# Mixer products halved panel by panel with more of them ahead of two waits, and seven squares in each down-projection sweep

## The chip, the cores and the metric

The kernel runs on one core of a Trainium2 chip. That core has five engines that each run their own list of instructions: TensorE (PE in the profile; PEld is its loading of the stationary operand), VectorE (DVE), ScalarE (ACT), GpSimd (POOL) and SyncE (SP), which here only issues DMAs. They wait for each other through semaphores. PE reads SBUF and writes PSUM, which has eight banks of 512 floats in each of 128 partitions; ACT and DVE read PSUM and write SBUF.

The metric is the time of one execution in microseconds, the median over several runs. One per cent of the time before is 12.1 us.

## The reference

One layer of a decoder trunk on 256 tokens of width 2048. A mixer with two kinds of heads, a squared-ReLU MLP of width 8192, and a gated embedding:

```python
h = rms_norm(x, attn_norm)
z = h @ w_in                         # 4096 + 288 columns
zs = token_shift(z[pool part left out], mu_shift)
pool_out = (windowed means of z_pool, minus z_pool) @ pool_w * pool_scale
rwkv_out = rwkv7_time_mix(r, k, v, w, a, g from zs)
x = x + concat(pool_out, rwkv_out) @ w_out
h2 = rms_norm(x, mlp_norm)
x = x + square(relu(h2 @ w_ffn_up)) @ w_ffn_down
gate = sigmoid(rms_norm(x, ple_norm) @ w_ple_gate)
x = x + gate * (p @ w_ple_proj)
return rms_norm(x, final_norm)
```

The time mixing has a recurrence over tokens, S = S diag(w) + (S a) b^T + v k^T, y = S r, for 16 heads of 64. All is float32.

## The kernel before

**Products in parts.** A float32 product is made of three matmuls on rounded parts. A weight panel of 128 x 1024 (two k-tiles of 512 columns) is loaded as `raw`, ACT writes its rounded high part `wh` (two operations of 512 columns) and DVE the rest, `wl = raw - wh` (one operation of 1024 columns); this is `split_w`, L160 to 167. With activations split the same way, a product is high x high, high x low and low x high. Panels live in rings of three buffers in the mixer, and of four from the MLP on (`ring`, L147). A panel is loaded again into a buffer when the last reader of the old one is done.

**The mixer, from 26 us of the profile on.** The order of PE's instructions is the written order here (`manual_schedule` for PE); ACT's and DVE's order is a planner's, which simulates the program and picks by priority. Eight products with `w_in` (zk0, zr0, zk1, zr1, zv0, zv1, zp0, zp1) are generators in one queue. Each step of a generator emits one small product and tells a nominal time: 0.36 us in `gemm_cols` (three matmuls of 256 columns, L177 to 180; 64 steps) and 0.68 in `gemm_toks` (three of 512, L187 to 189; 32 steps). `fill(us)` takes steps from the queue until so much nominal time is emitted, and `finish(gen)` until a generator is through. Between the fills stands the recurrence in chunks of 64 tokens, for two groups of eight heads: `rwkv_lora` and `rwkv_k` (keys, their norms with `rnq` and `rnb`, and the operand AR, L588 to 594), the scores (`sc`, L623, and for group 1 L652, in halves of two parts), `inverse` (31 steps of two DVE operations that invert 32 x 32 triangles), `rwkv_merge` (joins the 32-blocks to 64, `gm` L740 and `qm` L749, out of T1G), `rwkv_values`, and `rwkv_core`, four chunks each of which needs the one before (`us` L842, its copies UV L849 on ACT and L850 on DVE, the state L857, the outputs `dy` L870). `inverse` is itself a generator: `pace` emits one of its 38 pieces for every 1.0 us of queue time, and `while beside: fill(1.0)` runs it to its end ahead of the merge.

The panels of a queued product go one after the other, except at the ends: `apart` merges the first two panels and the last two (L191), and within a merged group all steps of output half 0 come before those of half 1. In between, each k-tile goes through half 0 and half 1 in turn. When half 0 of the last group is complete, `consume` reads its PSUM bank out (`shift_evac`: ACT L332, DVE L333, for four pieces). Products share three PSUM banks, so the next product's half 1 takes the bank of this one's half 0.

Behind the core: `pool_chunk`, the first token half's group_out, `fill(4.0)`, the second one's (`yt` L902), the gates of each group with `fill(3.0)` behind them, pool products, then `w_out` (`o_b`).

**The MLP.** `gemm_wide` makes 512 hidden units at a time (`u_w`), `square` squares them and keeps them as activations. `ffn_half` does eight of these, 16 pairs of k-tiles, and then two sweeps over `w_ffn_down`, each for 1024 output columns; so there are four sweeps of 16 pairs. A plain pair is 2 x 2 blocks of outputs with two k-tiles: 8 products, 24 matmuls of 512 columns. For the pairs in `SEVEN` the 2 x 2 block product is done with seven products (a Strassen-Winograd scheme, 21 matmuls): `square_seven` makes sums of activations, `weights_seven` sums of weight panels on DVE and their splits (L1226 to 1243). `sweep` (L1254) sums into eight PSUM banks p1 to p7 and d22; at the last seven-pair, 13, p1, p5, p6 and p7 are combined on DVE and added to the residual (L1285 to 1292, L1306). From the MLP on, the planner orders PE too.

**The end.** Embedding products, transposes, three gate products during which eight panels of the fourth are split and kept (`keep`), the fourth, and the final norm.

## Time and profile before

| | us |
|---|---|
| three runs | 1209.35, 1201.73, 1210.58; median 1209.35 |
| the profiled execution | 1204.18 |
| its span, first to last instruction | 1202.5 |
| mean granted clock of PE | 0.994 |
| PE busy | 1170.1 |
| DVE busy | 847.7 |
| ACT busy | 664.7 |
| mean DMA rate | 180 GB/s |

All busy times are unions over the span. A matmul's recorded time holds its way through the array, 0.28 us for 256 columns where the next one starts 0.12 us later, so rates are read from start to start. Lists of waits give the engine, the line and tile that waited, what ended the wait, and us in total, the number of times and the longest. Rows of windows give the stretch, its length, busy time and instructions of PE, PEld, DVE, ACT and POOL, the granted clock of PE (1.00 is full), the DMA share and GB/s. Rows of a timeline give start, length, engine, line, operation, out<-in, and in brackets the idle time before it and what ended it; where several instructions stand in a row (x4), start and length are those of all.

### The profile page before, as it was taken

The numbers are of one execution on the slowest core, as the hardware profiler recorded it, in microseconds if no ns is written. First come the engines' busy times: TensorE is split into PE (matmuls) and PEld (weight loads), VectorE is DVE, ScalarE is ACT, GpSimd is POOL, SyncE is SP. The second block draws the span as 40 slices with busy tenths as digits, with TensorE's granted clock in tenths as the row PEclk, the third lists the DMA queues.
The fourth block names the chain that finished last, engine by engine and source line by source line (L and its number), as shares of the span: only waits on it lengthen the run. The fifth ranks groups of instructions, "written<-read, shape, count | busy, mean of one in ns | idle before, by whom it ended". The sixth has DMA issues, their size and how long they took to land.

```text
span 1202.5 us, 18959 instructions
## 1 busy us (share of the span) xinstructions
PE 1170.1 (97%) x7378; PEld 1001.5 (83%) x7378; DVE 847.7 (70%) x1111; ACT 664.7 (55%) x1198; POOL 19.1 (2%) x77
## 2 busy tenths in 40 slices
PE   7899899999999999999999999999999999999997
PEld 6899898878887888888887888888888888877886
DVE  6785698557655666666879788666667788788753
ACT  5946555557554645555555554555545554568743
POOL 4100000000000000000000000000000000000000
PEclk9999899999999999999999999999999999999999
DMA  7353344445656666565656657556655666666741
GB/s 265 122 169 124 133 128 137 138 139 176 193 179 189 177 191 183 186 191 179 192 189 204 200 186 231 184 188 189 182 190 177 203 198 195 228 202 200 259 152 70
DMA packets 60618, 216.92 MB, mean 180 GB/s; under 512 B 6768, under 2 KB 7536, under 8 KB 60144
## 3 DMA queue, kind: packets, MB, share of 16 engines
q1 hardware_dynamic: 60240, 215.20, 55.8%
q8 instruction: 58, 0.95, 0.3%
q10 hardware_dynamic: 288, 0.51, 0.1%
q14 instruction: 32, 0.26, 0.1%
HBM read 213.59 MB, written 2.10 MB: 179 GB/s over the span
## 4 chain that ended last, share of the span: by engine, by line
PE 76%; DVE 11%; DMA 6%; ACT 4%; issue 2%; DVEq 0%; ACTq 0%
PE u_w L1115 20%; PE u_w L1119 10%; PE d_p L1185 9%; DMA raw_d<-in_w_ffn_down_dram 5%; PE d_w L1185 3%; PE o_b L189 2%; PE o_b L188 2%; PE o_b L187 2%; PE d_d L1185 2%; PE gt_b L188 2%; PE gt_b L187 2%; PE gt_b L189 2%; DVE wl_d L166 1%; PE wag_b L369 1%; PE zp_b L187 1%
## 5 line engine op out<-in xcount | busy, mean ns | idle before, releaser
L1115 PE MATMUL u_w<-h,wh_u 128*128 128x512 f32 x1024 | 362.1, 399 | 0.0
L1119 PE MATMUL u_w<-h,wl_u 128*128 128x256 f32 x1024 | 287.7, 281 | 0.0
L165 ACT ACTIVATE wh_u<-raw_u 128x512 fp32r<-128x512 f32 x256 | 147.7, 624 | 174.5 <-issue 133.3
L166 DVE TENSOR_TENSOR wl_u<-raw_u,wh_u 128x1024 fp32r<-128x1024 f32 x128 | 156.5, 1224 | 122.2 <-ACT wh_u L165 122.2
L1115 PEld LDWEIGHTS u_w<-h,wh_u 128*128 128x128 f32 x1024 | 192.5, 188 | 48.0
L1119 PEld LDWEIGHTS u_w<-h,wl_u 128*128 128x128 f32 x1024 | 193.4, 189 | 0.0
L1185 PE MATMUL d_p<-wh_d,yd 128*128 128x512 f32 x480 | 154.6, 390 | 0.6 <-DVE x L1306 0.5
L165 ACT ACTIVATE wh_d<-raw_d 128x512 fp32r<-128x512 f32 x160 | 89.1, 620 | 36.0 <-issue 16.7
L1185 PEld LDWEIGHTS d_p<-wh_d,yd 128*128 128x128 f32 x480 | 90.1, 188 | 20.0 <-ACT wh_d L165 1.3
L166 DVE TENSOR_TENSOR wl_d<-raw_d,wh_d 128x1024 fp32r<-128x1024 f32 x80 | 95.5, 1220 | 13.5 <-ACT wh_d L165 13.1
L1185 PE MATMUL d_p<-wl_d,yd 128*128 128x512 f32 x240 | 93.9, 391 | 0.8 <-DVE wl_d L166 0.8
L166 DVE TENSOR_TENSOR wl_o<-raw_o,wh_o 128x1024 fp32r<-128x1024 f32 x32 | 39.1, 1224 | 34.6 <-ACT wh_o L165 34.6
L1185 PE MATMUL d_d<-wh_d,yd 128*128 128x512 f32 x160 | 55.8, 389 | 0.0
L165 ACT ACTIVATE wh_o<-raw_o 128x512 fp32r<-128x512 f32 x64 | 36.7, 624 | 33.3 <-PE o_b L189 18.2
L1185 PEld LDWEIGHTS d_p<-wl_d,yd 128*128 128x128 f32 x240 | 45.0, 188 | 11.7 <-DVE wl_d L166 2.6
L1238 ACT ACTIVATE th_d<-t_d 128x1024 fp32r<-128x1024 f32 x24 | 25.4, 1059 | 46.0 <-DVE t_d L1235 40.1
L1185 PE MATMUL d_w<-th_d,ys 128*128 128x512 f32 x144 | 48.2, 389 | 0.0
L1242 ACT ACTIVATE th_d<-t_d 128x1024 fp32r<-128x1024 f32 x24 | 25.4, 1059 | 35.1 <-DVE t_d L1240 35.1
L1243 DVE TENSOR_TENSOR tl_d<-t_d,th_d 128x1024 fp32r<-128x1024 f32 x24 | 29.4, 1224 | 19.9 <-ACT th_d L1242 19.6
L1232 ACT ACTIVATE w7h_d<-raw_d 128x1024 fp32r<-128x1024 f32 x24 | 25.4, 1059 | 26.3 <-PE d_p L1185 11.5
L178 PE MATMUL zr_b<-hTh,wh_zr 128*128 128x256 f32 x128 | 38.5, 301 | 1.2 <-ACT wh_zr L165 1.2
L180 PE MATMUL zr_b<-hTh,wl_zr 128*128 128x256 f32 x128 | 37.7, 294 | 2.0 <-DVE wl_zr L166 2.0
(530 smaller groups left out, 2544.0 us busy)
## 6 DMA issues: line engine op xcount, KB each, us to landing
raw_u<-in_w_ffn_up_dram SPq DMA_DIRECT2D x128, 512.0 KB, 3.5
raw_d<-in_w_ffn_down_dram SPq DMA_DIRECT2D x128, 512.0 KB, 4.1
raw_o<-in_w_out_dram SPq DMA_DIRECT2D x32, 512.0 KB, 3.5
raw_gt<-in_w_ple_gate_dram SPq DMA_DIRECT2D x24, 512.0 KB, 4.4
raw_zk<-in_w_in_dram SPq DMA_DIRECT2D x16, 512.0 KB, 4.1
raw_zr<-in_w_in_dram SPq DMA_DIRECT2D x16, 512.0 KB, 3.5
raw_zv<-in_w_in_dram SPq DMA_DIRECT2D x16, 512.0 KB, 3.5
raw_zp<-in_w_in_dram SPq DMA_DIRECT2D x16, 512.0 KB, 3.5
```

What stands on the lines that cost most here:

```text
L165: nc.scalar.activation(wh[:, a * 512 : (a + 1) * 512], raw[:, a * 512 : (a + 1) * 512], AF.Copy)
L166: nc.vector.tensor_tensor(wl, raw, wh.bitcast(F32), op=ALU.subtract)
L178: nc.tensor.matmul(o, w_h, ah, start=first and ct % 2 == 0, stop=False, skip_group_check=True)
L180: nc.tensor.matmul(o, w_l, ah, start=False, stop=last, skip_group_check=True)
L187: nc.tensor.matmul(o, a_h, wh[:, 0:n], start=first, stop=False)
L188: nc.tensor.matmul(o, a_h, wl[:, 0:n], start=False, stop=False)
L189: nc.tensor.matmul(o, a_l, wh[:, 0:n], start=False, stop=last)
L1115: nc.tensor.matmul(bank[:, ct, :].rearrange("p (s t) -> p s t", s=2), wh[:, c], hl, start=k == 0, stop=False, skip_group_check=True,)
L1119: nc.tensor.matmul(bank[:, ct, 0:T], wl[:, c], hl[:, 0, :], start=False, stop=k == 15, skip_group_check=True)
L1185: nc.tensor.matmul(o, l, r, start=first, stop=last, skip_group_check=True)
L1232: nc.scalar.activation(ha, ra, AF.Copy)
L1243: nc.vector.tensor_tensor(tl[1], t[1], th[1].bitcast(F32), op=ALU.subtract)
```

## The change

- **Panel by panel.** `apart` goes. In `gemm_cols` every panel is emitted half by half: its two k-tiles for output half 0, then for half 1. In `gemm_toks` with `split_ends` every panel's steps are ordered by token half. At the end, half 0 is complete four steps (two in `gemm_toks`) ahead of the product's end instead of eight (four).
- **More product ahead.** `fill(7.0)` ahead of group 1's first scores becomes 12.0, a `fill(2.4)` is added ahead of the merge, and in each of the core's four chunks 2.4 behind `us` becomes 2.8. The queue is the same.
- **Copies.** In the merge all copies out of PSUM go to ACT (before: group 0's ACT, group 1's DVE), and the four copies of the diagonal blocks to DVE at high priority. In the core UV of group 1 goes to ACT as well.
- **Seven squares.** `SEVEN` is 1, 3, 5, 7, 9, 11, 13 instead of 2, 4, 7, 9, 11, 13. Seven-squares' activations get seven buffers of their own, plain ones go two to a large slot.
- **Wider sums.** The weights of `w_ffn_down` are laid out in DRAM so that a pair's two loads hold b11, b22 and b12, b21. Then t1 and t3 are one operation of 1024 columns (b12 is subtracted from both), t2 and t4 stay 512 wide, and one subtraction of 2048 columns makes all four low parts. t1 has the other sign, so p5 is subtracted at pair 13, in one operation for two sums; the residual takes two operations of 1024 columns at lower priority (10000) instead of four of 512.
- **Low parts last.** In products of three matmuls, high x low-weight comes third instead of second; in a sweep's plain blocks and in p5, p7, p6, p4 all matmuls with high weights come before those with low weights.
- **Buffers.** t, th and tl are one tile of four 512s each; the kept gate panels and a few small tiles move to other tags.

```diff
-            nc.tensor.matmul(o, a_h, wl[:, 0:n], start=False, stop=False)
-            nc.tensor.matmul(o, a_l, wh[:, 0:n], start=False, stop=last)
+            nc.tensor.matmul(o, a_l, wh[:, 0:n], start=False, stop=False)
+            nc.tensor.matmul(o, a_h, wl[:, 0:n], start=False, stop=last)
...
+        for kp in range(nkp):
+            raw = load_raw(src[kp].rearrange("p a n -> p (a n)"), 1024, f"{name}_{kp}")
+            parts = split_w(raw, f"{name}_{kp}")
+            for half in range(2):
+                for a, (wh, wl) in enumerate(parts):
+                    k = 2 * kp + a
+                    ah, al = acts(k)
+                    for ct in (2 * half, 2 * half + 1):
+                        prod_cols(banks[half : half + 1], (ct * 128,), wh, wl, ah, al, k == 0, k == 2 * nkp - 1, ct % 2)
+                        yield 0.36
+                if kp == nkp - 1:
+                    consume(half, banks[half])
...
+            order_ = [(a, w, tt) for a, w in enumerate(split_w(raw, f"{name}_{kp}")) for tt in range(2)]
+            if split_ends:
+                order_.sort(key=lambda awt: awt[2])
...
-        def copy(i, dst, src):
+        def copy(dst, src):
             with tc.high_priority(30000):
-                if i:
-                    nc.vector.tensor_copy(dst, src)
-                else:
-                    nc.scalar.activation(dst, src, AF.Copy)
+                nc.scalar.activation(dst, src, AF.Copy)
...
-                for j, (a_, r, t_) in enumerate(sts[0]["parts"]):
-                    copy(j // 2, a_[r, :, t_], diag[r])
+                for a_, r, t_ in sts[0]["parts"]:
+                    with tc.high_priority(30000):
+                        nc.vector.tensor_copy(a_[r, :, t_], diag[r])
...
-                nc.vector.tensor_copy(flat3(UVs[1][c])[HI], us[HI, :])
-            fill(2.4)
+                nc.scalar.activation(flat3(UVs[1][c])[HI], us[HI, :], AF.Copy)
+            fill(2.8)
...
-    fill(7.0)
+    fill(12.0)
     rwkv_scores_half(1, st1, 0)
...
     while beside:
         fill(1.0)
+    fill(2.4)
     rwkv_merge(sts)
...
-    SEVEN = (2, 4, 7, 9, 11, 13)
+    SEVEN = tuple(range(1, 14, 2))
...
             nc.scalar.activation(ha, ra, AF.Copy)
+            nc.vector.tensor_tensor(
+                t[:, 0:2], ra.rearrange("p (c n) -> p c n", c=2), b12.unsqueeze(1).to_broadcast([128, 2, 512]), op=ALU.subtract
+            )
             nc.vector.tensor_tensor(la, ra, ha.bitcast(F32), op=ALU.subtract)
...
+            nc.scalar.activation(th[:, 0:2], t[:, 0:2], AF.Copy)
+            nc.vector.tensor_tensor(t[:, 2], b22, t[:, 0], op=ALU.add)
+            nc.vector.tensor_tensor(t[:, 3], b21, t[:, 2], op=ALU.subtract)
+            nc.scalar.activation(hb[:, 0:512], b21, AF.Copy)
+            nc.scalar.activation(th[:, 2:4], t[:, 2:4], AF.Copy)
+            nc.vector.tensor_tensor(lb[:, 0:512], b21, hb[:, 0:512].bitcast(F32), op=ALU.subtract)
+            nc.vector.tensor_tensor(tl, t, th.bitcast(F32), op=ALU.subtract)
...
+                for step in (put_high, put_low):
+                    for which, o, f, t in (
+                        ("p5", p5, F_S1, "t1"), ("p7", p7, F_S3, "t3"), ("p6", p6, F_S2, "t2"), ("p4", p4, F_A22, "t4")
+                    ):
+                        step(which, o, a(f), w[t], fin and which != "p4")
                 if fin:
+                    u = fp.tile([128, 4, 512], F32, tag="U", name=f"u_{name}")
+                    with tc.high_priority(30000):
+                        nc.scalar.activation(u[:, 0], p1, AF.Copy)
+                        nc.vector.tensor_tensor(u[:, 1], p6, u[:, 0], op=ALU.add)
+                        nc.vector.tensor_tensor(u[:, 2], p7, u[:, 1], op=ALU.add)
+                        nc.vector.tensor_tensor(
+                            u[:, 1::2], u[:, 1:3], p5.unsqueeze(1).to_broadcast([128, 2, 512]), op=ALU.subtract
+                        )
+                    for tt in range(2):
+                        residual_(n0, tt, u[:, 2 * tt : 2 * tt + 2].rearrange("p c n -> p (c n)"), 1024)
             else:
+                (b11, b22), (b12, b21) = (split_w(r, f"{name}_{j}_{i}") for j, r in enumerate((ra, rb)))
+                ws = [(b11, b21), (b12, b22)]
                 for which, o, tt, b in (("p2", p2, 0, 0), ("p3", p3, 0, 1), ("p4", p4, 1, 0), ("d22", d22, 1, 1)):
+                    for step in (put_high, put_low):
+                        for j in range(2):
+                            step(which, o, acts[i](tt, j), ws[b][j], end and j == 1)
...
+        with tc.high_priority(10000 if wide > 512 else 30000):
```

More of the change, by code (lines that the diff above doesn't have):

```diff
@@ L740, in rwkv_merge @@
                     nc.tensor.matmul(b[low, u * 32 : u * 32 + 32], a_[top, uu, 32:64], T1G[top, uu, :], start=True, stop=True)
-            for i, (a_, top, low) in enumerate(pairs):
-                copy(i, T1G[low, hf * 16 : hf * 16 + 16].rearrange("t u j -> t (u j)"), b[low, :])
+            for a_, top, low in pairs:
+                copy(T1G[low, hf * 16 : hf * 16 + 16].rearrange("t u j -> t (u j)"), b[low, :])
             fill(1.4)
@@ L1267, in put, with put_high, put_low @@
             begun.add(which)
+        def put_high(which, o, a, w, last):
+            mm(o, a[0], w[0], which not in begun, False)
+            mm(o, a[1], w[0], False, False)
+            begun.add(which)
+        def put_low(which, o, a, w, last):
+            mm(o, a[0], w[1], False, last)
         for i in range(npair):
@@ new lines, in sweep @@
+                for which, o, f, t in (("p1", p1, F_A11, "b11"), ("p2", p2, F_A12, "b21"), ("p3", p3, F_S4, "b22")):
+                    put(which, o, a(f), w[t], fin and which == "p1")
+                for step in (put_high, put_low):
[3 more added lines that the diff above has]
+                        step(which, o, a(f), w[t], fin and which != "p4")
@@ L1465, in _layout @@
         "w_ffn_up": halves(a["w_ffn_up"][0]),
-        "w_ffn_down": panels(a["w_ffn_down"][0]),
+        "w_ffn_down": squares(a["w_ffn_down"][0]),
         "w_ple_gate": panels(a["w_ple_gate"][0]),
```

143 lines of the change are left out of this document (48 added, 95 removed).

## The prediction

> **What bounds the kernel now.** First the page's busy table, then the list of whom TensorE (PE) waited for (us in total, times, longest).
>
> ```profile
> span 1202.5 us, 18959 instructions
> PE 1170.1 (97%) x7378; PEld 1001.5 (83%) x7378; DVE 847.7 (70%) x1111; ACT 664.7 (55%) x1198; POOL 19.1 (2%) x77
> ```
> ```profile
> PE wag_b L369 <- DMA wag<-in_w_wag_dram: 7.4, 1, 7.4
> PE sc L652 <- DVE AR L594: 4.2, 1, 4.2
> PE zr_b L180 <- DVE wl_zr L166: 2.0, 1, 2.0
> PE us L857 <- DVE UV L850: 2.0, 1, 2.0
> PE gm L740 <- DVE T1G L716: 1.9, 1, 1.9
> PE zr_b L178 <- ACT wh_zr L165: 1.2, 1, 1.2
> ...
> PE d_p L1185 <- DVE wl_d L166: 0.8, 2, 0.5
> PE zv_b L180 <- DVE wl_zv L166: 0.8, 1, 0.8
> ...
> PE rnb L499 <- DVE rnq L563: 0.6, 1, 0.6
> PE d_p L1185 <- DVE x L1306: 0.5, 1, 0.5
> ```
>
> PE is busy 97% of the span, so only two things pay: fewer matmuls, or less PE idle time. Behind the 7.4 us at the start (untouched), idle is small and lies nearly all in the mixer (zr, sc, us, gm, zv, rnb); the down-projection sweeps (d_p) show 1.3 us of it. Next the stretches by windows (the last columns but two are the granted clock) and PE's timeline around the longest wait.
>
> ```profile
> 56.00:60.00 4.00, 2.38 (x13) 2.38 (x14) 2.45 (x2) 3.97 (x8) 0.00 (x0) 0.77 0.34 113
> 60.00:64.00 4.00, 4.00 (x29) 3.96 (x28) 2.11 (x2) 2.04 (x5) 0.00 (x0) 0.80 0.47 154
> 140.00:144.00 4.00, 4.00 (x35) 3.88 (x35) 0.72 (x2) 0.00 (x0) 0.00 (x0) 0.51 0.36 123
> 144.00:148.00 4.00, 4.00 (x25) 3.87 (x23) 1.18 (x3) 0.61 (x2) 0.00 (x0) 0.64 0.00 0
> 150.00:200.00 50.00, 49.13 (x441) 47.43 (x441) 47.47 (x97) 28.88 (x58) 0.00 (x0) 1.00 0.42 137
> ...
> 250.00:260.00 10.00, 8.05 (x159) 6.17 (x159) 6.43 (x10) 6.01 (x15) 0.00 (x0) 1.00 0.33 107
> ```
> ```profile
> 131.90 0.28 PE L178 MATMUL zr_b<-hTh,wh_zr 128*128 128x256 f32 x1
> 132.26 0.28 PE L178 MATMUL zr_b<-hTh,wh_zr 128*128 128x256 f32 x1
> ...
> 139.82 3.48 PE L652 MATMUL sc<-AR,BK 64*128 64x64 f32 x32 [4.17 <-DVE AR L594]
> 143.24 0.58 PE L178 MATMUL zr_b<-hTh,wh_zr 128*128 128x256 f32 x1
> ...
> 146.81 0.33 PE L179 MATMUL zr_b<-hTl,wh_zr 128*128 128x256 f32 x1
> ...
> 158.09 2.00 PE L652 MATMUL sc<-AR,BK 64*128 64x64 f32 x32
> ```
>
> Two stretches run at a lower clock, each behind idle time: 56 to 64 us behind the waits of 1.2 and 2.0 on zr's splits, 140 to 148 behind the 4.2. A three-matmul product takes 0.36 us (131.90 to 132.26), 0.12 a matmul. From 143.24 to 146.81 lie 16 matmuls: 3.57 us instead of 1.92. The same 32 score matmuls take 3.48 us behind the wait and 2.00 at 158 us. So the wait of 4.2 costs 4.2 + 1.5 + 1.6 = 7.3 us. The single waits of 1.9 (gm, 200 us) and 2.0 (us, 258 us) have no slow stretch behind them: the window around the latter shows clock 1.00. [...]
>
> **Seven squares instead of six.** One pair of panels in each of four sweeps goes from 8 products of 3 matmuls to 7. From the chain of waits, and DVE's timeline in a sweep:
>
> ```profile
> 698.19 4.76 PE d_p L1185 x21
> ...
> 1030.27 4.36 DMA raw_d<-in_w_ffn_down_dram
> ```
> ```profile
> 680.56 4.62 DVE L166 TENSOR_TENSOR wl_d<-raw_d,wh_d 128x1024 fp32r<-128x1024 f32 x4
> 688.36 0.68 DVE L1235 TENSOR_TENSOR t_d<-raw_d 128x512 f32<-128x512 f32 x1
> 688.97 0.68 DVE L1239 TENSOR_TENSOR t_d<-raw_d,t_d 128x512 f32<-128x512 f32 x1
> ```
>
> 21 matmuls in 4.76 us are 0.227 us each; 4 x 3 x 0.227 = **2.7 us** saved, all on PE. DVE pays 1.15 us for a 1024-wide operation and 0.61 for a 512-wide one. A seven-pair costs it 3 x 1.15 + 5 x 0.61 = 6.5 us now; with the wider sums 2 x 1.15 + 3 x 0.61 + one of 2048 columns, not shown, between 2.2 (twice the step from 512 to 1024 on top of 1.15) and 2.3 (two of 1024): 6.4. A plain pair costs 2.3. A seven and a plain pair take PE 45 x 0.227 = 10.2 us and DVE 8.7, so PE sets the pace, as it does now where pairs 7, 9, 11 and 13 alternate with plain ones. The sums at pair 13 cost 8 x 0.61 = 4.9 us now and 2 x 0.61 + 3 x 1.15 = 4.7 then, and the two wide ones yield to the splits. Low halves come last: the first panel's split gets three more matmuls (0.7 us), the second's two fewer (0.45). The waits of 0.8 and 0.5 may go or grow: I take zero, between -1.5 and +1.5.
>
> **Fill moved forward.** Mixer products are a queue of 6 x 64 steps of 0.36 us and 2 x 32 of 0.68, 181.8 us; fills take from it in the written order, rounded up to whole steps, and I count with that. Ahead of group 1's scores 12 us instead of 7 are taken, 14 steps more: PE, which stopped at 135.7 and stood until 139.8, comes at 140.7. DVE may get one more split (1.15 us) ahead of AR, and zr1's evacuation falls there too, so I leave 0.8 us of new wait: 7.3 - 0.8 = **6.5 us**, between 4.2 and 7.3.
>
> At the merge 137.2 us of the queue are done instead of 130.3; from the second part of those scores to there 41.8 instead of 40.0. DVE works 47.5 of 50 us in this stretch, so it sets when T1G is ready. PE comes 1.8 us later relative to it, DVE loses zr1's evacuation and gains two thirds of a split: **1.6 us** of the 1.9, between 0 and 1.9.
>
> In the core both UV copies go to ACT. Its timeline and DVE's at the wait:
>
> ```profile
> 257.59 0.63 ACT L170 ACTIVATE pws<-raw_pw 128x512 fp32r<-128x512 f32 x1 [3.18 <-DMA raw_pw<-in_pool_w_dram]
> 258.13 0.57 ACT L849 ACTIVATE UV<-us 64x512 f32<-64x512 f32 x1
> ```
> ```profile
> 258.97 0.69 DVE L850 COPY UV<-us 64x512 f32<-64x512 f32 x1
> ```
>
> That wait is no load of DVE's: ACT stood 3.2 us before a weight DMA with UV queued behind it, then DVE. On ACT alone it can recur; only the 0.4 us of extra fill is sure. **1.0 us**, between 0 and 2. The merge's copies, two of 0.6 us in turn on ACT instead of side by side, lie under 1.4 us of fill; uncovered they cost 0.6 us a time.
>
> What is spent early is missing late: when the core ends, 13 steps of the queue (8.8 us) are left now, 2 steps (1.4) then. PE's timeline behind the core, DVE's last norm, and a window:
>
> ```profile
> 272.10 1.15 PE L870 MATMUL dy<-UV,SC 128*64 128x64 f32 x32
> ...
> 280.14 1.03 PE L902 MATMUL yt<-ident,ys 128*128 128x128 f32 x8
> ...
> 294.69 0.39 PE L187 MATMUL o_b<-wh_o,mg 128*128 128x512 f32 x1
> ```
> ```profile
> 278.80 0.69 DVE L896 TENSOR_TENSOR ys<-ys,gv 128x512 f32<-128x512 f32 x1
> ```
> ```profile
> 280.00:290.00 10.00, 10.00 (x55) 7.87 (x55) 8.97 (x13) 8.65 (x21) 0.00 (x0) 1.00 0.32 105
> ```
>
> The core's last matmuls end at 273.2, the last normalised ys at 279.5, 6.3 us later. Of the 6.9 us up to yt, 4.1 were product; with 1.4 PE stands at yt after 4.2: a new wait of 2.1. From yt to o_b lie 14.6 us, 4.8 of them product; without these 9.8 are left for the same evacuations. **-2.3 us**, between -1 (one split of 1.15 fewer in the way) and -6.9 (2.1 + 4.8).
>
> **Panel by panel.** Merged end groups went half by half over two panels; now each panel does. PE's timeline, and the window of the next boundary but one:
>
> ```profile
> 52.32 0.28 PE L178 MATMUL zr_b<-hTh,wh_zr 128*128 128x256 f32 x1
> ...
> 57.62 0.39 PE L180 MATMUL zr_b<-hTh,wl_zr 128*128 128x256 f32 x1 [2.04 <-DVE wl_zr L166]
> ```
> ```profile
> 110.00:120.00 10.00, 10.00 (x86) 8.90 (x79) 5.80 (x8) 9.95 (x23) 0.00 (x0) 1.00 0.19 60
> ```
>
> zr0 began at 52.32 us and needed panel 1 after 4 products (1.44 us); its wl was ready at 57.6. With 8 products of panel 0 ahead, 1.4 us of the two waits go and one below 2 us stays, which trips no clock at gm or us. The slow stretch costs between 0.5 (29 matmuls in 4 us where 33 fit) and 1.7 ((0.23 + 0.20) x 4); I count 1.2. Together **2.6 us**, between 1.0 and 2.9. Against it, a gemm's first half is complete 1.44 us before its end instead of 2.9. For zk1 its evacuation falls where ACT is busy 9.95 of 10 us, ahead of rnq: that wait of 0.6 grows, **-1.0 us** (0 to -2). At zv0's end DVE is full: **-0.5 us** (0 to -1.5).
>
> **Sum.** 2.7 + 6.5 + 1.6 + 1.0 - 2.3 + 2.6 - 1.0 - 0.5 = 10.6 us. The profiled execution took 1204.2 us (1.7 around its span): 1193.6. The three runs' median, 1209.35, lies 5.2 us above it: 1198.8. I forecast the middle, **1196 us**; rivals are reckoned from the same middle.
>
> **Rivals.**
> 1. *The tail dries out* (0.20). If the 21.5 us from 273.2 to 294.7 are the evacuations' own, all 7.4 us of product taken earlier come back as waits, not 2.3; if they also slow the clock, 3 us more, as at 140. Gain 2.5 to 5.5: 1201 to 1204. For it: DVE is busy 9.0 and ACT 8.7 of 10 us there. Against: some of that is splits which move forward. [...]
> 2. *The wait moves to the merge* (0.14). If DVE's work ahead of T1G ends no earlier, some 4 us of the scores' gain come back at gm: 1200.
> 3. *Slower* (0.08). In a sweep a panel's buffer is loaded again when its last reader is done. A seven-pair's buffers turn once in 10.2 us: 4.4 of DMA (1030.27) and nearly 6 of readers. If the 2048-wide subtraction is put ahead of the second panel's low split, that buffer stays about 1 us longer; beyond some 0.5 us PE starves. 7 x 4 pairs x 1 us = 28: 1224. Against: in the written order readers are fewer and the subtraction is last.
>
> That the squares save nothing is excluded by their count.
>
> **Numbers.** The forecast has 0.58. The range 1184 to 1208 reaches from all good ends (17 us off the fastest run, 1201.7) to the dry tail on the median with its clock; rival 3 stays outside. Within 1%, about what a measurement of this kernel can tell from no change, means above 1197.3: of the forecast some 0.6 lies below (0.35), of rivals 1 and 2 a third (0.11). Faster 0.46, same 0.46, slower 0.08.
>
> **What would show it.** Right: no wait above 1 us at sc L652 and clock 1.00 from 130 to 150; gm's wait under 1; a new wait of about 2 at yt L902; 12 matmuls fewer at 0.227 and idle below 2 us in the sweeps. Wrong: waits above 5 us from yt to o_b with a clock below 1; gm waiting 4; PE waiting on raw_d's splits once per seven-pair.

## The result, and the profile after

The changed kernel takes **1193.26 us** in the median of four runs (1192.45 to 1194.95), beside 1205.92 for four runs of the kernel before on the same chip. The ratio is **0.990, with a 95% interval of 0.9872 to 0.9929**. The profiled execution took 1192.48 us against 1204.18, its span is 1190.8 us against 1202.5, and the mean granted clock 0.997 against 0.994. The forecast was 1196 us with a range of 1184 to 1208, and 1193.6 for the profiled execution.

First the page's span and busy table of the changed kernel, with the group of the new 2048-column subtraction (line, engine, operation, tiles, count, busy us, mean ns, idle before it).

```profile
span 1190.8 us, 18955 instructions
PE 1164.7 (98%) x7366; PEld 996.4 (84%) x7366; DVE 855.4 (72%) x1073; ACT 678.7 (57%) x1210; POOL 20.1 (2%) x77
...
L1236 DVE TENSOR_TENSOR tl_d<-t_d,th_d 128x2048 fp32r<-128x2048 f32 x28 | 64.2, 2292 | 29.3 <-ACT th_d L1234 29.3
```

PE has the 12 matmuls fewer that the squares save, and 5.4 us less busy time. That is more than 12 x 0.227 = 2.7, since matmuls at a lower clock count as longer: in the kernel before's slow stretch behind zr's splits (0.50 from 58.5 to 61.5 us) those of 256 columns are 0.41 us long and start 0.21 apart, instead of 0.28 and 0.12. The new subtraction takes 2.29 us, the upper of the two bounds given (2.2 and 2.3).

Next the list of whom PE waited for (total, times, longest).

```profile
PE wag_b L359 <- DMA wag<-in_w_wag_dram: 7.8, 1, 7.8
PE d_p L1173 <- DVE wl_d L166: 2.8, 6, 0.6
PE zr_b L178 <- DVE zk_t L323: 2.0, 1, 2.0
PE sc L642 <- DVE AR L584: 1.4, 1, 1.4
PE zv_b L178 <- DVE zv_t L323: 1.3, 1, 1.3
PE yt L890 <- DVE gv L883: 1.2, 1, 1.2
...
PE yt L890 <- DVE ys L884: 0.2, 1, 0.2
```

The waits at gm (1.9), us (2.0) and rnb (0.6) are gone. The one at sc has shrunk from 4.2 to 1.4, and those on zr's splits (2.0 and 1.2) have become a single wait of 2.0 on another step: `zk_t` L323 reads the product before out of its PSUM bank. New are the waits at yt, and the sweeps wait more for wl_d (2.8 in six instead of 0.8 in two).

PE's timeline shows what stands behind these waits (start, duration, line, operation, tiles; the bracket gives the idle time before).

```profile
56.59 0.39 PE L178 MATMUL zr_b<-hTh,wh_zr 128*128 128x256 f32 x1 [1.99 <-DVE zk_t L323]
...
139.19 2.00 PE L642 MATMUL sc<-AR,BK 64*128 64x64 f32 x32 [1.39 <-DVE AR L584]
...
141.46 0.34 PE L180 MATMUL zv_b<-hTh,wl_zv 128*128 128x256 f32 x1
...
144.79 0.36 PE L178 MATMUL zv_b<-hTh,wh_zv 128*128 128x256 f32 x1
...
175.99 0.39 PE L178 MATMUL zv_b<-hTh,wh_zv 128*128 128x256 f32 x1 [1.34 <-DVE zv_t L323]
...
276.28 0.63 PE L890 MATMUL yt<-ident,ys 128*128 128x128 f32 x4 [1.22 <-DVE gv L883]
...
286.43 0.39 PE L187 MATMUL o_b<-wh_o,mg 128*128 128x512 f32 x1
```

The scores take 2.00 us now (3.48 before), but the products behind them are slow from 141.46 to 144.79, although the wait was only 1.39. The first matmul of the output product (o_b) starts at 286.43 instead of 294.69. The windows tell the same of the clock (the last columns but two).

```profile
56.00:60.00 4.00, 3.42 (x28) 3.42 (x29) 2.35 (x4) 3.98 (x10) 0.00 (x0) 1.00 0.31 116
140.00:144.00 4.00, 4.00 (x37) 3.93 (x36) 3.99 (x6) 0.81 (x2) 0.00 (x0) 0.69 0.72 211
144.00:148.00 4.00, 4.00 (x46) 3.79 (x46) 1.78 (x3) 1.15 (x2) 0.00 (x0) 0.88 0.13 53
280.00:290.00 10.00, 10.00 (x62) 8.18 (x59) 8.98 (x16) 6.75 (x16) 0.00 (x0) 1.00 0.13 45
```

Read off PE's timelines, the 11.7 us between the two spans come from these stages: up to o_b 8.3 us, from there to the first sweep 0.3, in the sweeps (start of the first down-projection matmul to start of the last) 1.1, and 2.0 between there and the first gate product (15.42 us before, 13.42 after). In that last stretch PE waited 2.1 us before (pp_b 0.8 and 0.5, h3t 0.8) and 0.6 after (h3t).

### The profile page after: what moved, and what is told of

It reads as the page before. It is cut to its first block, busy times and chain, and to the rows that moved or that the text cites. A ratio compares the mean times of both kernels' runs of the same rounds, so it can differ in the third digit from the quotient of the medians.

```text
span 1190.8 us, 18955 instructions
## 1 busy us (share of the span) xinstructions
PE 1164.7 (98%) x7366; PEld 996.4 (84%) x7366; DVE 855.4 (72%) x1073; ACT 678.7 (57%) x1210; POOL 20.1 (2%) x77
## 4 chain that ended last, share of the span: by engine, by line
PE 73%; DVE 5%; DMA 2%; ACT 1%; issue 1%; DVEq 0%; ACTq 0%
PE u_w L1104 20%; PE d_p L1173 13%; PE u_w L1108 10%; PE d_w L1173 5%; PE d_d L1173 3%; PE o_b L188 2%; PE o_b L187 2%; PE o_b L189 2%; PE gt_b L187 2%; PE gt_b L189 2%; PE gt_b L188 2%; DVE wl_d L166 2%; DMA raw_d<-in_w_ffn_down_dram 2%; PE zp_b L187 1%; PE zp_b L189 1%
## 5 line engine op out<-in xcount | busy, mean ns | idle before, releaser
L165 ACT ACTIVATE wh_u<-raw_u 128x512 fp32r<-128x512 f32 x256 | 147.4, 624 | 175.6 <-issue 136.7
L1173 PE MATMUL d_p<-wh_d,yd 128*128 128x512 f32 x432 | 115.6, 389 | 0.0
L1173 PEld LDWEIGHTS d_p<-wh_d,yd 128*128 128x128 f32 x432 | 81.0, 188 | 16.6
L165 ACT ACTIVATE wh_d<-raw_d 128x512 fp32r<-128x512 f32 x144 | 79.7, 619 | 23.4 <-PE d_d L1173 12.0
L166 DVE TENSOR_TENSOR wl_d<-raw_d,wh_d 128x1024 fp32r<-128x1024 f32 x72 | 85.1, 1219 | 2.3 <-ACT wh_d L165 2.2
L1236 DVE TENSOR_TENSOR tl_d<-t_d,th_d 128x2048 fp32r<-128x2048 f32 x28 | 64.2, 2292 | 29.3 <-ACT th_d L1234 29.3
L1173 PE MATMUL d_p<-wl_d,yd 128*128 128x512 f32 x216 | 68.5, 393 | 2.8 <-DVE wl_d L166 2.8
L1234 ACT ACTIVATE th_d<-t_d 128x1024 fp32r<-128x1024 f32 x28 | 29.7, 1060 | 69.1 <-DVE t_d L1232 69.1
L1226 DVE TENSOR_TENSOR t_d<-raw_d,raw_d 128x1024 f32<-128x1024 f32 x28 | 34.2, 1222 | 14.4 <-DMA raw_d<-in_w_ffn_down_dram 14.4
L1230 ACT ACTIVATE th_d<-t_d 128x1024 fp32r<-128x1024 f32 x28 | 29.7, 1060 | 17.9 <-DVE t_d L1226 14.7
L178 PE MATMUL zv_b<-hTh,wh_zv 128*128 128x256 f32 x128 | 37.8, 295 | 1.3 <-DVE zv_t L323 1.3
L1173 PE MATMUL d_d<-wh_d,yd 128*128 128x512 f32 x144 | 38.5, 389 | 0.0
## 6 DMA issues: line engine op xcount, KB each, us to landing
raw_u<-in_w_ffn_up_dram SPq DMA_DIRECT2D x128, 512.0 KB, 3.5
raw_d<-in_w_ffn_down_dram SPq DMA_DIRECT2D x128, 512.0 KB, 4.4
raw_o<-in_w_out_dram SPq DMA_DIRECT2D x32, 512.0 KB, 3.5
raw_gt<-in_w_ple_gate_dram SPq DMA_DIRECT2D x24, 512.0 KB, 4.4
raw_zk<-in_w_in_dram SPq DMA_DIRECT2D x16, 512.0 KB, 4.1
raw_zr<-in_w_in_dram SPq DMA_DIRECT2D x16, 512.0 KB, 3.5
raw_zv<-in_w_in_dram SPq DMA_DIRECT2D x16, 512.0 KB, 3.5
raw_zp<-in_w_in_dram SPq DMA_DIRECT2D x16, 512.0 KB, 3.5
```

The costliest lines, as they stand in the source:

```text
L165: nc.scalar.activation(wh[:, a * 512 : (a + 1) * 512], raw[:, a * 512 : (a + 1) * 512], AF.Copy)
L166: nc.vector.tensor_tensor(wl, raw, wh.bitcast(F32), op=ALU.subtract)
L178: nc.tensor.matmul(o, w_h, ah, start=first and ct % 2 == 0, stop=False, skip_group_check=True)
L1173: nc.tensor.matmul(o, l, r, start=first, stop=last, skip_group_check=True)
L1226: nc.vector.tensor_tensor(t[:, 0:2], ra.rearrange("p (c n) -> p c n", c=2), b12.unsqueeze(1).to_broadcast([128, 2, 512]), op=ALU.subtract)
L1230: nc.scalar.activation(th[:, 0:2], t[:, 0:2], AF.Copy)
```

## The experiments

All kernels compute the whole layer. The ratios are to the kernel before. For the mixer one figure more is taken from each trace: the time from the first zr product to o_b, which leaves out the start-up's DMA. It was 242.4 us before and is 233.4 after. It is taken from one execution of each kernel, and a slow stretch of the clock more or less moves it by up to 1.7 us, an estimate from the granted clocks of after_again at 56 to 64 us, (0.34 + 0.08) x 4: that is the changed kernel once more, with one such stretch more.

| kernel | median, us | ratio, 95% | zr to o_b, us | sweeps, us |
|---|---|---|---|---|
| before (profiled) | | | 242.4 | 516.1 |
| changed (profiled) | 1193.26 | 0.9900 (0.9872 to 0.9929) | 233.4 | 515.0 |
| mixer_only | 1196.82 | 0.9923 (0.9894 to 0.9952) | 233.5 | 515.8 |
| mlp_only | 1206.26 | 0.9985 (0.9964 to 1.0006) | 246.7 | 515.1 |
| fills_only | 1194.95 | 0.9905 (0.9881 to 0.9930) | 234.5 | 514.5 |
| panels_only | 1203.21 | 0.9967 (0.9946 to 0.9988) | 242.9 | 515.9 |
| fill7 | 1195.67 | 0.9909 (0.9883 to 0.9934) | 238.5 | 513.2 |
| fill16 | 1203.01 | 0.9966 (0.9951 to 0.9981) | 242.1 | 514.3 |
| last_merged | 1199.86 | 0.9921 (0.9896 to 0.9946) | 242.9 | 516.0 |
| after_again | 1194.97 | 0.9886 (0.9865 to 0.9908) | 234.9 | 514.7 |
| no_prefill | 1192.72 | 0.9869 (0.9847 to 0.9890) | 232.4 | 514.6 |
| pairs_low | 1191.38 | 0.9855 (0.9832 to 0.9878) | 233.4 | 512.6 |
| best12 | 1188.66 | 0.9854 (0.9826 to 0.9882) | 232.6 | 512.0 |
| best14 | 1189.45 | 0.9856 (0.9831 to 0.9881) | 232.7 | 513.6 |

### The two halves of the change

Theory: the mixer's edits bring most of the gain. Rival: the sweeps' edits do, or they take back what the mixer wins.

mixer_only is the kernel before with all of the mixer's hunks (panels, fills, copies, the mixer's low parts last); SEVEN and the sums stay:

```diff
-    fill(7.0)
+    fill(12.0)
...
+    fill(2.4)
     rwkv_merge(sts)
...
     SEVEN = (2, 4, 7, 9, 11, 13)
```

> The mixer's part of the change alone, the MLP as before. Theory (the two parts add up, and the mixer's gain is made ahead of o_b): o_b starts 8 to 9 us earlier than before (294.7 us there, 286.4 in the changed kernel), the same waits as in the changed kernel at zr (2.0), sc (1.4), zv (1.3) and yt (1.4); the whole is 8 to 9 us faster than before. Rival (much of what is gained in the mixer is made possible by the MLP's part or lost behind it): less than 6 us or more than 10.

mlp_only is the kernel before with the rest:

```diff
-    SEVEN = (2, 4, 7, 9, 11, 13)
+    SEVEN = tuple(range(1, 14, 2))
...
     fill(7.0)
     rwkv_scores_half(1, st1, 0)
```

> The MLP's part alone (seven squares, wider sums, low halves last, buffers), the mixer as before. Theory: 2.7 us from 12 matmuls fewer, 2 us of it lost again to waits on wl_d (2.8 us instead of 0.8), 1 to 2 us won at the end of the last sweep: 1 to 3.5 us faster than before. Rival (the waits on wl_d come from the mixer's part, by other alignment): waits on wl_d below 1 us, 3.5 to 5 us faster.

The mixer alone wins 0.77%, the sweeps alone 0.15% with an interval that includes no change. Beside one another the two ratios make 0.9923 x 0.9985 = 0.991, and the whole change was measured at 0.990: the halves add up, within intervals of 0.2 to 0.3% to either side. mixer_only's profiled execution took 8.8 us less than that of the kernel before, as the theory had it, but its median 10.8 us less, which is more than the 10 at which the rival began. The rival's reason did not show: the mixer's waits are those expected, and the MLP's part is not there to help. mlp_only's waits are those of the kernel before in the mixer (sc 4.2, gm 1.9, us 2.0) and those of the changed kernel in the sweeps (wl_d 2.3 in five).

### The mixer's edit taken apart

Once last_merged (below) had lost 5 us, I took the panels for the main cause. These two kernels, each with one half of the mixer's edit on the kernel before, were to decide between that and the prediction's terms.

panels_only:

```diff
-        for group in apart(nkp, True):
+        for kp in range(nkp):
...
     fill(7.0)
     rwkv_scores_half(1, st1, 0)
```

> The kernel before with the products' halving alone: every panel half by half, low part of the activation ahead of the weight's; the fills, the copies and the sweeps as before. By the terms of the prediction (2.6 - 1.0 - 0.5) it wins 1.1 us: 1206 to 1207 beside a kernel before at 1207 to 1208 in the same call. New theory, from the run in which merging the last two panels again cost 5 us: taking panels singly is worth 4 to 6 us, because the second half of a z product is read out earlier and the chain of ScalarE and VectorE work to AR ends 3 to 5 us sooner: 1201 to 1204, with the first score matmul of group 1 at 139 to 140 us only if product stands ahead of it; without the added product the wait at sc stays at 3.5 to 5 us and with it a clock below 0.8 at 140 to 148.

fills_only:

```diff
         for group in apart(nkp, True):
...
-    fill(7.0)
+    fill(12.0)
     rwkv_scores_half(1, st1, 0)
...
+    fill(2.4)
     rwkv_merge(sts)
```

> The kernel before with the other half of the mixer's edit alone: 12 instead of 7 us of product ahead of group 1's scores, 2.4 ahead of the merge, 2.8 instead of 2.4 in the core, and the copies moved between ScalarE and VectorE; the products' end groups over two panels as before. By the terms of the prediction (6.5 + 1.6 + 1.0 - 2.3) it wins 6.8 us: 1200 to 1202. New theory: more splits and read-outs go ahead of AR on VectorE, which comes 3 to 5 us later, so the wait at sc stays at 3 us or more and its slow clock too; it wins 0 to 4 us: 1203.5 to 1208.

The new theory held for one half and fell for the other. In the times panels_only wins 0.33% (1203.2 us), inside the theory's 1201 to 1204 and more than the 1.1 us of the prediction's terms. fills_only wins 0.95%, where the theory had the scores' wait stay and the prediction's terms had 6.8 us. Both together (mixer_only) win no more than the fills alone, so the two gains do not add up in the times.

In panels_only's profiled execution the way from zr to o_b is not shorter (242.9 us against 242.4). Its list of waits, and its windows at the merge:

```profile
PE sc L642 <- DVE AR L584: 4.9, 1, 4.9
PE zr_b L178 <- DVE zk_t L323: 2.0, 1, 2.0
PE us L847 <- DVE UV L840: 1.5, 1, 1.5
PE gm L730 <- DVE T1G L706: 1.3, 1, 1.3
PE sc L642 <- DVE AR L589: 1.1, 1, 1.1
```
```profile
200.00:204.00 4.00, 4.00 (x112) 3.73 (x110) 3.94 (x5) 2.71 (x3) 0.00 (x0) 0.75 0.41 135
204.00:208.00 4.00, 4.00 (x58) 3.71 (x55) 2.06 (x4) 1.74 (x3) 0.00 (x0) 0.50 0.34 125
208.00:212.00 4.00, 4.00 (x138) 3.83 (x134) 1.49 (x2) 0.59 (x1) 0.00 (x0) 0.90 0.45 131
```

AR was ready at 136.7 us there, three earlier than in the kernel before. PE came 3.7 us earlier, so it stood from 132.0 on, 0.7 us longer than before, and the clock fell behind the wait as before (0.64 and 0.50 at 136 to 144 us); another 1.1 us went at the next part of the scores. Ahead of a wait whose releaser isn't moved as far, time won on PE becomes waiting time. At the first gm matmul 2.1 us of the lead were left (147.6 us behind the first zr product instead of 149.7). They were lost in the merge, where the clock was below 1 in three windows of 4 us that ran at 1.00 in the kernel before's profiled execution.

That clock is a matter of the execution. mlp_only, whose mixer is that of the kernel before, ran from 200 to 216 us at 0.91, 0.50, 0.50 and 0.81 and took 246.7 us from zr to o_b. An estimate without it: one minus the granted clock, times the length of the window, summed from zr to o_b, is the most that the clock can have cost. It is 5.1 us in the kernel before, 10.2 in mlp_only, 6.8 in panels_only, 3.4 in fills_only and 1.7 in mixer_only. Less that, the way takes 237.3, 236.4, 236.1, 231.1 and 231.8 us. The first two have the same mixer, so about 1 us is this reading's error. By it the panels alone win 1.2 us and the fills and copies 6.2, close to the prediction's 1.1 and 6.8, and the panels on top of the fills win nothing. How much of panels_only's 0.33% is fewer slow stretches was not settled; its ten runs go from 1199.8 us at a mean clock of 0.994 to 1207.9 at 0.991.

fills_only had no wait at the scores at all. Its list of waits, and the window that had 0.51 before:

```profile
PE zr_b L180 <- DVE wl_zr L166: 2.0, 1, 2.0
PE yt L900 <- DVE gv L893: 1.4, 1, 1.4
PE zr_b L178 <- ACT wh_zr L165: 1.2, 1, 1.2
```
```profile
140.00:144.00 4.00, 4.00 (x45) 3.87 (x45) 3.94 (x7) 2.60 (x6) 0.00 (x0) 1.00 0.69 221
```

The two waits on zr's splits stand as they were, and there the clock still falls (0.69 and 0.50 at 56 to 64 us). mixer_only, with the panels, has a wait of 1.4 at the scores again. In the times fills_only and mixer_only can't be told apart (0.9905 and 0.9923, with intervals of a quarter per cent to either side).

### How much product ahead of the scores

```diff
-    fill(12.0)
+    fill(7.0)
     rwkv_scores_half(1, st1, 0)
```

That is fill7; fill16 is the same with `fill(16.0)`.

> The changed kernel with 7.0 instead of 12.0 us of product ahead of group 1's scores. Theory (that product fills a wait that is set by DVE's chain to AR): the wait at sc is 4 us again with a granted clock near 0.5 behind it, so 3 us more there and 2 us more of slow matmuls; 1.4 us come back at yt, where product is left again: 3 to 4 us slower than the changed kernel. Rival (product is only shifted, the wait returns elsewhere): within 1 us of it.

> The changed kernel with 16.0 instead of 12.0. Theory (the slow clock at 140 us follows PE's idle time): no wait at sc, clock 1.00 from 140 to 148 us, which is 1.4 + 1.4 us better; the tail has 4 us of product less, the wait at yt grows from 1.4 to between 2.5 and 5: between 1.5 us faster and 1 us slower than the changed kernel. Rival (the scores, small matmuls, lower the clock by themselves): clock below 0.95 there without a wait.

With 7 the wait is back. With 16 the wait and the slow clock are gone, and the kernel is nevertheless 0.7% slower than the changed one. fill16's windows and waits:

```profile
140.00:144.00 4.00, 3.96 (x40) 3.83 (x42) 3.99 (x6) 1.98 (x4) 0.00 (x0) 1.00 0.72 205
...
204.00:208.00 4.00, 3.67 (x9) 2.81 (x9) 3.57 (x6) 1.56 (x3) 0.00 (x0) 0.50 0.15 60
...
284.00:288.00 4.00, 3.81 (x14) 2.71 (x15) 2.66 (x5) 3.43 (x10) 0.00 (x0) 0.63 0.00 0
```
```profile
PE zp_b L187 <- DVE zv_t L323: 3.6, 1, 3.6
PE yt L890 <- DVE gv L883: 2.6, 1, 2.6
```

The expectation had between 1.5 us faster and 1 us slower. The queue is so far ahead that zv1 ends before the merge. Its four read-outs (L323) fall into the stretch in which DVE is full with T1G and the copies out of it; zp0 needs the banks and waits 3.6 us, the clock falls to 0.50, and gm starts at 208.5 instead of 200.1. The core waits another 1.5 us for its UV copy on ACT (dy). The yt wait has grown to 2.6, as less of the queue is left for it, and the clock falls behind it too. The theory of the scores' wait was right, and the rival wrong: the scores ran at a clock of 1.00 once they did not wait. What the theory left out is the wait at zp: more product ahead of the scores is not better without end.

fill7's list has sc at 4.9 + 1.1, and o_b comes 5.1 us later than in the changed kernel. In the times that is only 0.1% (0.9909 to 0.9900, within the intervals), a good deal less than the 3 to 4 us expected. That is the rival's time without the rival's reason, as the wait came back where it had been. Its sweeps were 1.8 us shorter in the profiled execution; where the rest went was not settled.

### The products' end

```diff
-        for kp in range(nkp):
+        for group in [(i,) for i in range(nkp - 2)] + [(nkp - 2, nkp - 1)]:
...
-                for a, (wh, wl) in enumerate(parts):
-                    k = 2 * kp + a
+                for k, (wh, wl) in parts:
```

> In the changed kernel the last two panels of each z product are taken half by half together again, the others stay panel by panel. Theory: the waits of 2.0 at zr and 1.3 at zv are the read-out of the product before, whose first half is complete only 1.44 us before its end when panels go singly; with 2.9 us they shrink to under 0.7 each, and 2 to 3 us are won: 1190 to 1191 beside the changed kernel's 1192.5 to 1195 (ratio to it 0.998). Rival: the two waits are only the place where the mixer's DVE work shows, which stays the same; then they are named after another step (the last split's wl, or T1G, or AR) and the time stays within 1 us of the changed kernel's.

It was 4.9 us slower than the changed kernel beside it (after_again, 1194.97). The read-out waits did go: zr waits 1.8 on a split again and zv not at all. But the scores wait 4.2, and the theory's gain is lost several times over. DVE's timeline ahead of AR's last step in the changed kernel:

```profile
136.21 1.20 DVE L581 SCALAR_TENSOR_TENSOR AR<-tB_t,tA_t 128x1008 f32<-128x1008 f32 x1
137.33 1.22 DVE L166 TENSOR_TENSOR wl_zv<-raw_zv,wh_zv 128x1024 fp32r<-128x1024 f32 x1
138.47 0.48 DVE L323 SCALAR_TENSOR_TENSOR zr_t<-zr_b,par_sb,zr_t 128x255 f32<-128x255 f32 x1
138.86 0.18 DVE L584 TENSOR_SCALAR AR<-tB_t 128x16 f32<-128x16 f32 x1
```

and in last_merged:

```profile
139.39 1.20 DVE L582 SCALAR_TENSOR_TENSOR AR<-tB_t,tA_t 128x1008 f32<-128x1008 f32 x1
140.50 0.48 DVE L324 SCALAR_TENSOR_TENSOR zr_t<-zr_b,par_sb,zr_t 128x255 f32<-128x255 f32 x1
140.89 1.22 DVE L166 TENSOR_TENSOR wl_zv<-raw_zv,wh_zv 128x1024 fp32r<-128x1024 f32 x1
142.03 0.48 DVE L324 SCALAR_TENSOR_TENSOR zr_t<-zr_b,par_sb,zr_t 128x255 f32<-128x255 f32 x1
142.42 1.22 DVE L166 TENSOR_TENSOR wl_zv<-raw_zv,wh_zv 128x1024 fp32r<-128x1024 f32 x1
143.55 0.48 DVE L324 SCALAR_TENSOR_TENSOR zr_t<-zr_b,par_sb,zr_t 128x255 f32<-128x255 f32 x1
143.94 0.17 DVE L585 TENSOR_SCALAR AR<-tB_t 128x16 f32<-128x16 f32 x1
```

The last step of AR takes 0.17 us and is the one that PE waits for. It starts 5.1 us later. Two splits and three read-outs stand between it and the step before it, 3.4 us, where the changed kernel has one of each in 1.5: that is 1.9 us of the 5.1. The other 3.2 were lost before: rnq, the norms that the chain to AR needs, came at 126.5 instead of 123.5 us, behind a slow stretch at 59 to 62 us (0.86 and 0.71 at 56 to 64 us) that this execution had and the changed kernel's had not (1.00). The late AR is not a property of merged ends as such, as fills_only shows, which has them too and doesn't wait. The two timelines suggest the order that the planner gives DVE, together with that slow stretch; neither was changed by itself.

### What the changed kernel leaves

> The changed kernel once more, unedited, as the measure for the three edits of it that run beside it. 1192.4 to 1195 us as in its four runs, the profile with the same list of waits: zr 2.0, sc 1.4, zv 1.3, yt 1.2, wl_d 2.8 in six.

This is the measure for the next two: 1194.2 to 1196.4 us beside them, in part above what was expected. The waits are nearly the same; the profiled execution has one slow stretch more, at 57 to 61 us, and took 1.7 us longer than the first.

```diff
-                for which, o, tt, b in (("p2", p2, 0, 0), ("p3", p3, 0, 1), ("p4", p4, 1, 0), ("d22", d22, 1, 1)):
+                blocks = (("p2", p2, 0, 0), ("p3", p3, 0, 1), ("p4", p4, 1, 0), ("d22", d22, 1, 1))
+                for group in (blocks[0:2], blocks[2:3], blocks[3:4]):
...
-                        for j in range(2):
-                            step(which, o, acts[i](tt, j), ws[b][j], end and j == 1)
+                        for which, o, tt, b in group:
+                            for j in range(2):
+                                step(which, o, acts[i](tt, j), ws[b][j], end and j == 1)
```

> In the changed kernel the plain pairs take the high parts of the products with the first panel and with the second panel (p2, p3) ahead of the low parts of both, so that the second panel's low half is first needed at the tenth matmul (2.0 us) instead of the sixth (1.1 us). Theory: the waits of 2.8 us in six on the down-projection's wl come from that order alone and fall to below 1; 1 to 2.5 us won: 1190 to 1193. Rival: the split itself comes late because the raw panel lands late (its buffer is held longer by the seven-squares' wide sums); then the wait moves with it, 2 us or more stay, and the time does not change.

pairs_low takes 1189.8 to 1192.9, all below after_again's runs, 3.6 us in the median. Its list of waits has this for the sweeps:

```profile
PE pp_b L187 <- DVE x L1312: 1.1, 1, 1.1
PE d_p L1173 <- DVE wl_d L166: 0.6, 2, 0.4
```

The sweeps take 512.6 us instead of 515.0 and 514.7, and one new wait of 1.1 appeared behind them. So the order decides whether PE waits. The raw panels are late all the same, but for DVE. ACT's, DVE's and PE's timelines ahead of one of the waits in the changed kernel:

```profile
589.07 2.20 ACT L165 ACTIVATE wh_d<-raw_d 128x512 fp32r<-128x512 f32 x4
593.19 1.23 DVE L1226 TENSOR_TENSOR t_d<-raw_d,raw_d 128x1024 f32<-128x1024 f32 x1 [1.72 <-DMA raw_d<-in_w_ffn_down_dram]
594.33 2.35 DVE L166 TENSOR_TENSOR wl_d<-raw_d,wh_d 128x1024 fp32r<-128x1024 f32 x2
596.74 0.50 PE L1173 MATMUL d_p<-wl_d,yd 128*128 128x512 f32 x1 [0.64 <-DVE wl_d L166]
```

The plain pair's high halves were done at 591.3, so its two low halves could have been made from then on. DVE stood 1.7 us for the next seven-pair's panel instead and made that pair's sum first. Five of the six waits have this ahead of them, with DVE standing 1.25 to 1.7 us. In pairs_low DVE stands as long (14.8 us in 13 waits for raw_d, 14.4 in 13 in the changed kernel), and PE has four more matmuls to do meanwhile. Whether the plain pair's splits ahead of that sum would do as well was not tried. Nor does the turned order always suffice: best14 below has it and waits 1.9 in four.

```diff
-    fill(2.4)
     rwkv_merge(sts)
```

> The changed kernel without the 2.4 us of product ahead of the merge (its second added piece); the first, 12 instead of 7 ahead of the scores, stays. Theory by its trace: T1G was ready 4.7 us before the first gm matmul, so no wait appears at gm, and the 2.5 us of product that are left for behind the core take the waits of 1.2 + 0.2 at yt away: 0 to 1.5 us won, 1191.5 to 1194. Rival: DVE sets when T1G is ready and PE comes 2.5 us earlier against it; with the loss of cover a wait of up to 1.9 comes back at gm, in some executions with a granted clock below 1 in the merge, and the time rises by 1 to 5 us with a spread as wide as that of the kernel before.

No wait came back at gm: the granted clock was 1.00 from 196 to 208 us, and the last transposition into T1G had ended 4.7 us ahead of gm in the changed kernel (195.4 and 200.1). The waits at yt, and that at vt, are gone: what isn't spent ahead of the merge fills the tail. It takes 1192.1 to 1194.5, 2.2 us less than after_again in the median; one of its four runs lies within after_again's, and the intervals of the two ratios overlap.

best12 has these two edits; best14 has them and this one:

```diff
-    fill(12.0)
+    fill(14.0)
     rwkv_scores_half(1, st1, 0)
```

> The changed kernel with two edits that won singly: highs of p2 and p3 ahead of their lows in the plain pairs, and no product ahead of the merge. If the two gains (3.6 and 2.2 us against the changed kernel in the same call) lie in different stages, they add up: 1188.5 to 1190.5, with no wait above 0.5 at yt and wl_d waits below 1. Rival: part of each was the spread of executions; 1191 to 1193.

> As the run beside it, with 14 instead of 12 us of product ahead of group 1's scores, so that the queue stands at the merge where the changed kernel has it. Theory: with 2 us more of product the wait of 1.4 at sc and the clock below 1 behind it at 140 to 148 go (as with 16), while the read-out of zv1 doesn't fall ahead of the merge as with 16: 1.5 to 3 us better than the run beside it, 1186 to 1189. Rival: the splits and read-outs that the added product pulls ahead of AR on VectorE keep the wait at 1 us or more, and new waits appear at zp or zv (3.6 with 16): 1190 to 1196.

best12 takes 1188.66 us (1187.9 to 1191.1) beside 1207.29 for the kernel before, the lowest median of all and below every run of the changed kernel. Its ratio, 0.9854, can't be told from pairs_low's or best14's, so the times don't show that the two gains add up. In best14 the wait at the scores and its slow clock are gone (1.00 at 140 to 148 us) as the theory had it. The median lies between the theory's range and the rival's, but the rival described the rest, in best14's list of waits:

```profile
PE zv_b L178 <- DVE zr_t L323: 1.1, 1, 1.1
PE zv_b L178 <- DVE zv_t L323: 1.0, 1, 1.0
...
PE zp_b L187 <- DVE zv_t L323: 0.6, 1, 0.6
PE yt L890 <- DVE gv L883: 0.6, 1, 0.6
```

best12 had a wait of 1.4 at the scores and one of 1.3 at zv; these are four shorter ones on read-outs and norms with 3.3 us together, the waits on wl_d are 1.9 instead of 0.8, and nothing is won.

## Why the prediction was right, and where not

The direction, the stage and the size came out as the sum had them: 10.6 us were predicted between the profiled executions, 11.7 measured (10.0 with after_again's). The mechanism held: waits of PE in the mixer went, and the clock behind them rose. Term by term, from the two traces:

| term | predicted, us | measured, us |
|---|---|---|
| seven squares | 2.7 + 0 for stalls | 1.1 |
| scores | 6.5 | 4.3 |
| merge | 1.6 | 1.9 |
| UV in the core | 1.0 | 2.0 |
| tail | -2.3 | -1.4 |
| zr0's splits | 2.6 | 3.0 |
| rnb | -1.0 | +0.6 |
| end of zv0 | -0.5 | -0.5 |
| behind the sweeps | not seen | 2.0 |

The measured ones add up to 13.0; the first zr product began 0.7 us later (0.4 of it a longer wait at the start), and 0.6 stay unexplained. That the sum came so near is luck in part: squares and scores gave 3.8 us less than counted, and the core, rnb and the end of the sweeps 4.6 more. Two of the signs named for being right did not come: the scores still waited more than 1 us with a clock below 1 behind them, and PE idled more than 2 us in the sweeps.

**Squares.** The 12 matmuls went as counted. The stalls, taken as zero between -1.5 and +1.5, came out at the lower bound: PE's waits in the sweeps rose from 1.3 to 2.8. The step that failed is that with the low halves last "the second's two fewer (0.45)" would balance the first panel's gain; the second panel's low half was the late one, in the sixth matmul of a plain pair (596.74 above), and DVE had the next seven-pair's sum with its late panel in front of it. pairs_low shows that the place counts: with the order turned the waits are 0.6, and the sweeps are 3.5 us shorter than before instead of 1.1.

**Scores.** The wait lost 2.8 us (4.17 to 1.39) and the scores 1.5 (3.48 to 2.00). What failed is the 1.6 for the products behind: the prediction let the slow clock go with the long wait, as its author's estimate, but behind 1.39 us of idle time the products were still slow for 3.3 us. Also, 0.8 us of wait were left in the sum and 1.4 came, by one split and one read-out on DVE ahead of AR's last step, as was named.

**Merge and core.** Both waits went entirely. The merge's term was right in size, as a wait of 1.9 can give no more, but not in its reason. It had PE come 1.8 us later against DVE, and DVE nearly as before. Counted from the second part of the scores, PE did come 2.2 us later, but T1G was done after 49.7 us instead of 54.1. That left 4.7 us to spare, and no_prefill shows that the 2.4 us of product ahead of the merge were not needed. In the core ACT still stands 2.3 us before the weight DMA, but behind both UV copies (253.0 and 253.6 us, the weights at 256.5), so UV was not held up; whether the copy on ACT or the moved product did it wasn't tried apart.

**Tail.** The wait at yt came, 1.4 instead of 2.1. The share of the way from yt to o_b had been put at almost nothing, which held: no wait appears there and the clock is 1.00. Rival 1 would have had 7.4 us come back. It is not wrong in kind: with more product taken forward (fill16) the yt wait is 2.6 with a clock of 0.63 behind it, and without the 2.4 ahead of the merge (no_prefill) it is gone.

**Panels.** The wait that was left at zr0 is just as long as said, below 2 us, but it waits for the read-out of zk0, not for a split; the half that is complete later was named as a cost for zk1 and zv0 and forgotten for zk0. That the slow stretch went is the execution's luck: after_again had the same wait with 0.66 behind it. With 1.2 us less of waiting and about 1.7 of slow clock, the way from the first zr product to the first rnb went from 17.3 to 14.4 us. For rnb the sign was wrong. ACT and DVE were put in another order by the planner, rnq came at 123.5 instead of 127.1, and the wait vanished.

**From the profiled execution to the median.** The prediction took half of the 5.2 us between them. The median moved by more than the spans, since the changed kernel's runs lie within 2.5 us. Nineteen runs of the kernel before, beside mixer_only, go from 1203.4 us at a mean granted clock of 0.994 to 1210.0 at 0.989. mlp_only, which keeps the kernel before's waits, scatters likewise (1200.3 to 1208.9), and in its profiled execution the clock fell at the merge, behind the wait of 1.9 at gm (0.50 from 204 to 212 us). By an estimate from these the clock accounts for the spread: 0.994 less 0.989, times some 1206 us, is 6.0 of the 6.6 us. So much of that 5.2 was the price of slow stretches behind waits that the change removes or shortens, and they could have been put on its account. For the same reason the prediction's reading that waits of 1.9 and 2.0 trip no clock is true of the one execution it was read from.

**Rivals 2 and 3.** gm waits for nothing, and no panel's buffer starves the sweeps by 1 us a pair: the 2048-wide subtraction stands last of a seven-pair's work on DVE, as the written order has it.

## What to carry to other kernels

Put product ahead of a wait until the wait is gone, and then look at what the queue no longer has further on; both too little (fill7) and too much (fill16) show as a list of waits elsewhere. When an edit is judged, follow PE's gain to the next wait and see how far its releaser moved, since no more than that goes through (panels_only: 3.7 us became 2.9), and count the slow stretches of both executions before their spans are compared. And read the step that releases a wait together with what its engine has just ahead of it: two splits and three read-outs ahead of a step of 0.2 us in last_merged, and in the sweeps a sum that stood for a late panel while the split that PE needed was ready to run.

## What the runs showed of the hardware

The clock fell behind 1.39 and 1.27 us of idle time (both below), less than the 1.9 and 2.0 behind which the prediction saw no slow stretch, and not in every execution. The same kernel with the same wait of 2.0 us at zr had a clock of 1.00 from 56 to 60 us in one execution, shown above, and 0.66 in another (after_again, window):

```profile
56.00:60.00 4.00, 3.12 (x16) 3.12 (x17) 2.06 (x3) 3.43 (x9) 0.00 (x0) 0.66 0.38 131
```

The slow stretches added up here come in one length or a multiple of it. In windows of 0.5 us the granted clock within them is 0.50 (from 140.5 to 146.5 us in the kernel before, from 142.0 to 144.5 in the changed one). With 0.50 for all of them, a window of 4 us with a granted clock of 0.69 holds 0.31 x 4 / 0.5 = 2.5 us of slow time. So there are 3.4 us of it behind the scores in the changed kernel (0.69 and 0.88), as there are at 56 to 64 us in after_again (0.66 and 0.92); 6.8 behind the scores in the kernel before (0.51 and 0.64) and in panels_only's merge (0.75, 0.50 and 0.90); 10.2 in mlp_only's merge (0.91, 0.50, 0.50 and 0.81).

At the scores 1.39 us of idle time and 32 matmuls of 64x64 came ahead of such a stretch in the changed kernel; at panels_only's merge 1.27 and 64 of 32x32. Behind waits of 1.34 (zv) and 1.22 (yt) between larger matmuls the changed kernel's clock stayed at 1.00 (windows from 172 to 180 and from 276 to 284 us). With the small matmuls alone it stayed there too: in fills_only, fill16 and best14 the same scores ran without a wait at a clock of 1.00 (140 to 148 us). What makes the clock fall behind one wait and not behind another was not shown.
